# Second block's gates computed with the weights stationary, its attention and retention outputs transposed by background steps

## The chip, the cores and the metric

The kernel runs on one core of one Trainium2 chip. The metric is the device time of one execution in microseconds (us), the median of three runs. The engines are PE (matmuls), DVE (vector), ACT (scalar), POOL and SP (here mostly the queue that issues the weight DMAs).

## What is computed

The input is one sequence of 256 tokens with 1024 features. Two blocks with two layers each run one after the other, all in float32. The first block (a state space mixer and a dilated attention beside each other, then a feed-forward part) is not touched except for the sums of squares at its very end. A layer of the second block is:

```
h = rms_norm_2(x, norm_g[i])
proj = h @ w_in[i]
rq, rk, rv, rz, mq, mk, mv, mz = jnp.split(proj, cuts, axis=-1)     # 512 columns each
r_out = retention(rotary(rq), rotary(rk), rv, ret_norm_g[i])
r_out = jax.nn.silu(rz) * r_out
m_out = moba(rms_norm(mq), rms_norm(mk), mv, rel_bias)
m_out = jax.nn.silu(mz) * m_out
x = x + jnp.concatenate([r_out, m_out], axis=-1) @ w_out[i]
gate = jax.nn.sigmoid(rms_norm_2(x) @ w_ple_gate[i])
x = x + gate * rms_norm_2(p[i] @ w_ple[i], ple_norm_g[i])
```

The gates are the two factors `silu(rz)` and `silu(mz)`, 256 tokens by 512 features each.

## The kernel before

**Products in three parts.** Every large product is split for accuracy: each operand is a rounded high part and a low remainder, and three matmuls (high by high, high by low, low by high) are added in PSUM. The weights come from memory in 488 units of 128 x 1024 values, two units per DMA. ACT makes the high part `wh` of a unit (L154), DVE the low part `wl` (L157; POOL some of them in the first block). Three pairs of `wh` and `wl` exist, and a unit is split two units ahead of its use, so unit n+3 has to wait until PE is done with unit n.

**Two forms of a product.** `slab` (kind "B", L396 to L398 by way of `mmB_unit`) holds 128 tokens of the activations stationary and streams 512 columns of weights: 12 matmuls of 512 columns for a unit; the result has the tokens on the partitions. `pairA` (kind "A", L449 to L451) holds 128 x 128 weights stationary and streams 256 tokens: 24 matmuls of 256 columns for a unit; the result has the features on the partitions. `outT` (L433 to L435) is of the second kind as well, for the output products; its units go through the k blocks in the order (4, 6, 0, 2) for `w_out_2`, so that the first two units read features 512 to 1023 (attention), and the next two features 0 to 511 (retention).

**Order of the work.** The program's text gives an order, in which background steps (generators in `self.bg`) are advanced by one step after each unit (`tick`), and `drain` runs them to the end. A scheduler then orders each engine's instructions by its own estimate of times; on the chip each engine runs its list strictly in that order. PSUM has three banks for products (`mm`), three for small products (`ch`) and two for transposes (`tr`).

**Second half of a layer of the second block.** After the projections for queries, keys and values, `moba` (attention) and `retention` run as background steps and leave their results `ym` and `yr` with tokens on the partitions. The slab of section 7 gives the attention's gate `zm`, that of section 3 the retention's gate `zr`: for each half of the tokens ACT takes the tanh (L889), DVE makes the gate of it (L890). `gated` multiplies `ym` or `yr` by its gate on DVE (L996), transposes the product on PE, four 128 x 128 transposes (L385) for each half of the tokens, and splits it out of PSUM on ACT (L378) and DVE (L389) into the tiles `A` (attention) and `O` (retention), which `w_out_2` reads. For the attention this runs in the background of section 3's slab. For the retention everything is issued after the drain, straight ahead of `w_out_2`.

**Retention.** Two pairs of heads; for a pair: scores (L966, L967) into `ch` banks, decay on DVE (L969), three products a head (L976 to L978), statistics on DVE (L981, L982), a power on POOL (L371), normalising on DVE (L987) and the gain on POOL (L990).

**Norm at the end of the first block.** `Norm.part` adds squares of the features; the norm between the blocks has `first` set and keeps two such sums (n = 0 and n = 1). The last additions (f = 6) are on DVE (L206, L208). `factor` adds over the partitions on PE (L232), `broadcast` spreads the factor by PE (L223), and DVE applies it (L262).

Of the kernel before, what the change touches and what calls it, by code (L numbers as in the profile page):

```python
# [10 lines left out]
F32 = mybir.dt.float32  # L11
F32R = mybir.dt.float32r
BF16 = mybir.dt.bfloat16
AF = mybir.ActivationFunctionType
ALU = mybir.AluOpType
# [3 lines left out]
P = 128  # L19
S = 256  # L20
D = 1024
# [19 lines left out]
QK_BUFS = 4  # L41
# [15 lines left out]
def plan():  # L57

    u = []

    def slab(name, layer, k, c0, kind="B"):
        for r in range(k // 256):
            u.append((kind, name, layer, 256 * r, c0))

    def col(name, layer, c0, k=1024):
        for r in range(0, k, 1024):
            u.append(("A", name, layer, r, c0))  # L70

    def out(name, l):
        for i in range(len(blocks(name)) // 8):
            u.append(("K", name, l, i, 0))

    for l in range(DEPTH):
        out("w_ple_2", l)
    for l in range(DEPTH):
        for half in range(2):
            slab("w_in", l, D, C_V + 512 * half)  # L80
        for half in range(2):
            for c in (C_K, C_Q, C_Q + 1024, C_Q + 2048):
                for f in range(4):
                    col("w_in", l, c + 512 * half + 128 * f)
        for f in range(8):
            col("w_in", l, C_B + 128 * f)
        for g in range(4):
            for f in range(4):
                col("w_in", l, C_XS + 512 * g + 128 * f)
            for f in range(4):  # L90
                col("w_in", l, C_Z + 512 * g + 128 * f)
            for f in range(4 * (g % 2), 4 * (g % 2) + 4):
                if g < 2:
                    col("w_in", l, C_GA + 128 * f)
                else:
                    col("w_attn_branch", l, 128 * f)
        for f in range(8):
            col("w_in", l, C_GS + 128 * f)
        for f in range(8):
            col("w_ssd_branch", l, 128 * f, 2048)  # L100
        out("w_out", l)
        for p in range(2):
            slab("w_gate_up", l, D, 256 * p, "C")
        for p in range(2, NPAIR):
            for j in (0, 128):
                col("w_gate_up", l, 256 * p + j)
            for j in (0, 128):
                col("w_gate_up", l, FFN + 256 * p + j)
        out("w_down", l)
    for l in range(DEPTH):  # L110
        for s in (6, 4, 5):
            slab("w_in_2", l, D, 512 * s)
        for f in range(8):
            col("w_in_2", l, 128 * f)
        for s in (2, 7, 3):
            slab("w_in_2", l, D, 512 * s)
        out("w_out_2", l)
        out("w_ple_gate_2", l)
    return u


class Weights:
# [40 lines left out]
    def next(self, kind, name, layer, r, c0):  # L163
        assert self.plan[self.at] == (kind, name, layer, r, c0), (self.plan[self.at], (kind, name, layer, r, c0))
        self.split_to(self.at + LEAD)
        h, lo = self.hl.pop(self.at)
        self.at += 1
        w = 128 if kind in "AK" else 512
        return h.rearrange("p (k c) -> p k c", c=w), lo.rearrange("p (k c) -> p k c", c=w)


class Norm:
# [13 lines left out]
    def get(self, k):  # L186
        return self.uh[k // 4], self.ul[k // 4], k % 4
# [4 lines left out]
    def part(self, f, n=2):  # L192

        nc = self.net.nc
        h = self.h[:, f:f + 2, :]
        uh, ul = self.uh[f // 4][:, f % 4:f % 4 + 2, :], self.ul[f // 4][:, f % 4:f % 4 + 2, :]
        for n, (acc, new) in enumerate(self.sq):
            q = new if f else acc
            if n == 0:
                nc.scalar.activation(q, h, AF.Square)  # L200
            else:
                for i in range(2):
                    nc.scalar.activation(q[:, i, :], h[:, i, :], AF.Square,
                                         scale=self.first[0][:, f + i:f + i + 1])
            if f:
                (nc.vector if f == 6 else nc.gpsimd).tensor_tensor(acc, acc, new, ALU.add)  # L206
            if f == 6:
                nc.vector.tensor_tensor(acc[:, 0, :], acc[:, 0, :], acc[:, 1, :], ALU.add)  # L208
        if self.gain is None:
            self.net.split(uh, ul, h)  # L210
            return
        for i in range(2):
            g = self.gain[:, f + i:f + i + 1]
            nc.scalar.activation(uh[:, i, :], h[:, i, :], AF.Identity, scale=g)
            nc.vector.scalar_tensor_tensor(ul[:, i, :], h[:, i, :], g, uh[:, i, :].bitcast(F32), ALU.mult,
                                           ALU.subtract)
# [66 lines left out]
class Net:  # L283
# [117 lines left out]
    def slab(self, name, layer, c0, kk, get, kind="B"):  # L401

        n = kk // 256
        ps = [self.mm.tile([P, 512], F32, tag="mm", name="mm") for _ in range(2)]
        for j in range(n):
            hw, lw = self.w.next(kind, name, layer, 256 * j, c0)
            xh, xl, k0 = get(2 * j)
            for t in range(2):
                self.mmB_unit(ps[t], t, hw, lw, xh, xl, k0, j == 0, j == n - 1)
            self.tick()  # L410
        yield from enumerate(ps)
# [578 lines left out]
            nc.gpsimd.tensor_tensor(y[:, :, cs], y[:, :, cs], gain[:, None, cs].to_broadcast([P, 2, 256]), ALU.mult)  # L990
            yield

    def gated(self, y, z, yh, yl):

        for t in range(2):
            self.nc.vector.tensor_tensor(y[:, t, :], y[:, t, :], z[:, t, :], ALU.mult)  # L996
        yield
        for t in range(2):
            ps = self.transpose4([y[:, t, 128 * i:128 * i + 128] for i in range(4)])
            ts = slice(128 * t, 128 * t + 128)  # L1000
            self.split(yh[:, :, ts], yl[:, :, ts], ps.rearrange("p (i t) -> p i t", i=4))

    def ple(self, l):

# [43 lines left out]
    def block2(self, l, x, n1):  # L1048
        nc, a, sp = self.nc, self.a, self.sp
# [6 lines left out]
        def tile(tag, shape, bufs=1):  # L1056
            return sp.tile([P, *shape], F32, tag=tag, name="b2", bufs=bufs)

        qn, qm, qr = [n1.steps()], [], []
# [8 lines left out]
        getu = n1.getv  # L1068
        mk = tile("B1", [4, S])
        self.proj2(l, 5, getu, "k", mk, qm, hg[:, 1, :])  # L1070
        ym, yr = tile("xs", [2, 512], 2), tile("xs", [2, 512], 2)
# [6 lines left out]
        self.proj2(l, 2, getu, "v", rv)  # L1078
        qr.append(self.retention(rq, rk, rv, rg, yr))
        ys = [self.pair([P, 4, S], "O0", "O1"), self.pair([P, 4, S], "A0", "A1")]  # L1080
        zm = tile("A2", [2, 512])
        self.proj2(l, 7, getu, "z", zm)
        qm.append(self.gated(ym, zm, *ys[1]))
        zr = tile("A4", [2, 512])
        self.proj2(l, 3, getu, "z", zr)
        self.drain(qm, qr)
        qr.append(self.gated(yr, zr, *ys[0]))
        next(qr[0])
        e = [sp.tile([P, 4, S], F32, tag=f"B{t}", name="e") for t in range(2)]
        for t in range(2):  # L1090
            nc.sync.dma_start(e[t], self.es[l][:, 4 * t:4 * t + 4, :])
# [151 lines left out]
```

## Time and profile before

| what | value |
|---|---|
| median of 3 runs | 1578.91 us (1575.67 to 1579.48) |
| the profiled execution's own time | 1579.01 us |
| its span, first to last instruction | 1577.2 us |
| mean granted TensorE clock | 0.993 of full speed |
| PE busy | 1540.3 us, 98% of the span |
| DVE busy | 1160.2 us, 74% |
| ACT busy | 822.9 us, 52% |
| POOL busy | 463.6 us, 29% |

Times in the rows are counted from the span's start. The second block runs from about 1253 us to the end; its two layers take some 165 us each. A matmul's row has its start and its modelled length; matmuls overlap, so the pace of PE is read from the distance of two starts. What stands in square brackets at a row's end is the time that the engine was idle before it, and the instruction that ended the wait.

### The profile page before, as it was taken

The numbers are of one execution on the slowest core, as the hardware profiler recorded it, in microseconds if no ns is written. First come the engines' busy times: TensorE is split into PE (matmuls) and PEld (weight loads), VectorE is DVE, ScalarE is ACT, GpSimd is POOL, SyncE is SP. The second block draws the span as 40 slices with busy tenths as digits, with TensorE's granted clock in tenths as the row PEclk, the third lists the DMA queues.
The fourth block names the chain that finished last, engine by engine and source line by source line (L and its number), as shares of the span: only waits on it lengthen the run. The fifth ranks groups of instructions, "written<-read, shape, count | busy, mean of one in ns | idle before, by whom it ended". The sixth has DMA issues, their size and how long they took to land.

```text
span 1577.2 us, 28986 instructions
## 1 busy us (share of the span) xinstructions
PE 1540.3 (98%) x11912; PEld 1467.8 (93%) x11912; DVE 1160.2 (74%) x1760; ACT 822.9 (52%) x1268; POOL 463.6 (29%) x283
## 2 busy tenths in 40 slices
PE   8999999999999999999999999999999999999998
PEld 7999999889989999899998999998999979898988
DVE  7988998775676655668997886677565677788776
ACT  6545577454455444544466764455444554365433
POOL 4666266543000000075436565010000111111110
PEclk9999999999999999999999999999999999999999
DMA  8644444445545555654444455565555545355542
GB/s 306 230 171 153 170 161 167 150 151 206 187 161 187 187 188 187 214 188 161 147 161 148 173 192 194 189 208 197 187 188 186 173 156 183 136 186 175 180 139 96
DMA packets 42660, 280.65 MB, mean 178 GB/s; under 512 B 4864, under 2 KB 7040, under 8 KB 10016
## 3 DMA queue, kind: packets, MB, share of 16 engines
q1 hardware_dynamic: 40592, 267.20, 49.0%
q0 software_dynamic: 1936, 11.60, 1.9%
q8 instruction: 93, 1.52, 0.4%
q14 instruction: 39, 0.32, 0.1%
HBM read 274.53 MB, written 4.26 MB: 177 GB/s over the span
## 4 chain that ended last, share of the span: by engine, by line
PE 85%; DVE 9%; ACT 2%; issue 2%; POOL 1%; DMA 0%; DVEq 0%; SPq 0%; POOLq 0%; ACTq 0%
PE mm L449 17%; PE mm L451 16%; PE mm L450 16%; PE mm L434 6%; PE mm L435 6%; PE mm L433 6%; PE mm L397 4%; PE mm L396 4%; PE mm L398 4%; DVE wl L157 3%; PE ch L662 2%; PE tr L385 1%; ACT wh L154 1%; DVE acc L612 1%; DVE E L525 1%
## 5 line engine op out<-in xcount | busy, mean ns | idle before, releaser
L154 ACT CAST wh<-raw 128x1024 fp32r<-128x1024 f32 x488 | 511.0, 1049 | 587.2 <-PE mm L450 365.1
L157 DVE TENSOR_TENSOR wl<-raw,wh 128x1024 fp32r<-128x1024 f32 x456 | 603.8, 1327 | 273.4 <-ACT wh L154 270.6
L451 PE MATMUL mm<-uh,wl 128*128 128x256 f32 x2112 | 591.7, 280 | 3.8 <-DVE wl L157 3.7
L449 PE MATMUL mm<-uh,wh 128*128 128x256 f32 x2112 | 595.1, 282 | 0.0
L450 PE MATMUL mm<-ul,wh 128*128 128x256 f32 x2112 | 589.5, 279 | 0.0
L449 PEld LDWEIGHTS mm<-uh,wh 128*128 128x128 f32 x2112 | 398.8, 189 | 5.1 <-issue 3.8
L451 PEld LDWEIGHTS mm<-uh,wl 128*128 128x128 f32 x2112 | 397.5, 188 | 5.2 <-DVE wl L157 4.6
L450 PEld LDWEIGHTS mm<-ul,wh 128*128 128x128 f32 x2112 | 398.6, 189 | 0.4 <-issue 0.2
L206 POOL TENSOR_TENSOR nsq<-nsq 128x512 f32<-128x512 f32 x18 | 28.2, 1570 | 474.7 <-ACT nsq L200 407.7
L157 POOL TENSOR_TENSOR wl<-raw,wh 128x1024 fp32r<-128x1024 f32 x32 | 79.1, 2471 | 67.6 <-ACT wh L154 62.5
L433 PE MATMUL mm<-A,wh 128*128 128x256 f32 x288 | 81.5, 285 | 1.4 <-ACT wh L154 1.4
L435 PE MATMUL mm<-A,wl 128*128 128x256 f32 x288 | 81.3, 285 | 0.1
L397 PE MATMUL mm<-wl,nu 128*128 128x512 f32 x192 | 76.5, 400 | 2.7 <-DVE wl L157 2.6
L652 POOL TENSOR_TENSOR M<-M,cb 128x768 f32<-128x768 f32 x32 | 70.0, 2204 | 25.7 <-ACT M L651 17.7
L398 PE MATMUL mm<-wh,nu 128*128 128x512 f32 x192 | 75.3, 395 | 0.0
L396 PE MATMUL mm<-wh,nu 128*128 128x512 f32 x192 | 72.1, 398 | 3.0 <-DVE tg L825 2.2
L470 POOL TENSOR_TENSOR qT<-qT,rp 64x512 f32<-64x512 f32 x32 | 63.1, 1971 | 28.3 <-DVE rp L467 28.2
L612 DVE SCALAR_TENSOR_TENSOR acc<-mm,feat,acc 128x255 f32<-128x255 f32 (+1 forms) x144 | 67.2, 475 | 4.3 <-ACT acc L610 2.9
L469 POOL TENSOR_TENSOR qT<-qT,rot 64x512 f32<-64x512 f32 x32 | 57.2, 1786 | 43.4 <-ACT qT L465 43.4
L434 PE MATMUL mm<-A,wh 128*128 128x256 f32 x224 | 63.6, 285 | 0.0
L433 PEld LDWEIGHTS mm<-A,wh 128*128 128x128 f32 x288 | 55.1, 191 | 1.9 <-ACT wh L154 1.7
L435 PEld LDWEIGHTS mm<-A,wl 128*128 128x128 f32 x288 | 54.6, 191 | 0.6 <-DVE wl L157 0.6
(307 smaller groups left out, 3100.6 us busy)
## 6 DMA issues: line engine op xcount, KB each, us to landing
raw<-in_w_dram SPq DMA_DIRECT2D x243, 1024.0 KB, 4.8
abc<-scr POOLq DMA_DIRECT2D x8, 1024.0 KB, 5.4
es<-e POOLq DMA_DIRECT2D x4, 512.0 KB, 4.2
e<-es SPq DMA_DIRECT2D x4, 512.0 KB, 4.2
raw<-in_w_dram SPq DMA_DIRECT2D x2, 512.0 KB, 4.4
h<-in_xT_dram SPq DMA_DIRECT2D x2, 512.0 KB, 8.9
h<-in_xT_dram SPq DMA_DIRECT2D x1, 1024.0 KB, 4.8
hs<-h POOLq DMA_DIRECT2D x1, 1024.0 KB, 5.9
```

The costliest lines, as they stand in the source:

```text
L154: self.nc.scalar.copy(h, raw)
L157: eng.tensor_tensor(lo, raw, h.bitcast(F32), ALU.subtract)
L396: nc.tensor.matmul(ps, xh[:, k0 + k, ts], hw[:, k, :], start=start and k == 0, stop=False)
L397: nc.tensor.matmul(ps, xh[:, k0 + k, ts], lw[:, k, :], start=False, stop=False)
L398: nc.tensor.matmul(ps, xl[:, k0 + k, ts], hw[:, k, :], start=False, stop=stop and k == 1)
L433: nc.tensor.matmul(ps, hw[:, n % 8, :], xh[:, kx, :], start=opens, stop=False)
L434: nc.tensor.matmul(ps, hw[:, n % 8, :], xl[:, kx, :], start=False, stop=False)
L435: nc.tensor.matmul(ps, lw[:, n % 8, :], xh[:, kx, :], start=False, stop=left[f] == 0)
L449: nc.tensor.matmul(ps, hw[:, k, :], xh[:, kx, :], start=j == 0 and k == 0, stop=False)
L450: nc.tensor.matmul(ps, hw[:, k, :], xl[:, kx, :], start=False, stop=False)
L451: nc.tensor.matmul(ps, lw[:, k, :], xh[:, kx, :], start=False, stop=j == n - 1 and k == 7)
L612: nc.vector.scalar_tensor_tensor(acc[:, j, k:S], ps[:, j, 0:S - k], w[:, 3 - k:4 - k], acc[:, j, k:S], ALU.mult, ALU.add)
```

## The change

The gates are no longer made by `slab` but by `pairA`, two feature blocks at a time, so that they come out with the features on the partitions. `turned` is a new background step list: it transposes the ungated `ym` or `yr` (one half of the tokens a step) and copies it out of PSUM on ACT into `yT`. `gated` now appends `turned` to the queue, runs the two pairs of the gate's product, takes the tanh and makes the gate, drains the queue, multiplies the gate by `yT` and splits the result. It is called once for the attention (section 7) and once for the retention (section 3). The plan of the weights follows: sections 7 and 3 are laid out as columns instead of slabs, with the same number of units in the same place. Beside that, the last additions of the second sum of squares (n = 1) in the norm between the blocks move from DVE to POOL.

```diff
-        for s in (2, 7, 3):
-            slab("w_in_2", l, D, 512 * s)
+        slab("w_in_2", l, D, 1024)
+        for s in (7, 3):
+            for f in range(4):
+                col("w_in_2", l, 512 * s + 128 * f)
...
-                (nc.vector if f == 6 else nc.gpsimd).tensor_tensor(acc, acc, new, ALU.add)
+                (nc.vector if f == 6 and n == 0 else nc.gpsimd).tensor_tensor(acc, acc, new, ALU.add)
             if f == 6:
-                nc.vector.tensor_tensor(acc[:, 0, :], acc[:, 0, :], acc[:, 1, :], ALU.add)
+                (nc.gpsimd if n else nc.vector).tensor_tensor(acc[:, 0, :], acc[:, 0, :], acc[:, 1, :], ALU.add)
...
-    def gated(self, y, z, yh, yl):
-
-        for t in range(2):
-            self.nc.vector.tensor_tensor(y[:, t, :], y[:, t, :], z[:, t, :], ALU.mult)
-        yield
+    def turned(self, y, yT):
+
         for t in range(2):
             ps = self.transpose4([y[:, t, 128 * i:128 * i + 128] for i in range(4)])
-            ts = slice(128 * t, 128 * t + 128)
-            self.split(yh[:, :, ts], yl[:, :, ts], ps.rearrange("p (i t) -> p i t", i=4))
+            self.nc.scalar.copy(yT[:, :, 128 * t:128 * t + 128], ps.rearrange("p (i t) -> p i t", i=4))
+            yield
+
+    def gated(self, l, s, get, y, q, yT, yh, yl):
+
+        nc = self.nc
+        zs = []
+        q.append(self.turned(y, yT))
+        for f in (0, 2):
+            ps = self.pairA("w_in_2", l, 512 * s + 128 * f, D, get)
+            z = self.sp.tile([P, 2, S], F32, tag="qk", name="z", bufs=QK_BUFS)
+            nc.scalar.activation(z, ps, AF.Tanh, scale=0.5)
+            nc.vector.scalar_tensor_tensor(z, z, 1.0, ps, ALU.add, ALU.mult)
+            zs.append((f, z))
+        self.drain(q)
+        for f, z in zs:
+            nc.vector.tensor_tensor(z, z, yT[:, f:f + 2, :], ALU.mult)
+            self.split(yh[:, f:f + 2, :], yl[:, f:f + 2, :], z)
...
-        zm = tile("A2", [2, 512])
-        self.proj2(l, 7, getu, "z", zm)
-        qm.append(self.gated(ym, zm, *ys[1]))
-        zr = tile("A4", [2, 512])
-        self.proj2(l, 3, getu, "z", zr)
-        self.drain(qm, qr)
-        qr.append(self.gated(yr, zr, *ys[0]))
-        next(qr[0])
+        self.gated(l, 7, getu, ym, qm, tile("A2", [4, S]), *ys[1])
+        self.gated(l, 3, getu, yr, qr, tile("A4", [4, S]), *ys[0])
```

What the scheduler makes of it on PE, first layer, where the retention's output `yr` (tile b_14420) is transposed (c_80 holds the identity matrix). Before, it stands between the last matmul on `A` and the first on `O`:

```order
L433 MATMUL mm<-A_14858,wh 128x256
L434 MATMUL mm<-A_14859,wh 128x256
L435 MATMUL mm<-A_14858,wl 128x256
L385 MATMUL tr<-c_80,b_14420 128x128 x8
L433 MATMUL mm<-O_14856,wh 128x256 x4
L434 MATMUL mm<-O_14857,wh 128x256
```

After, the last four of the eight transposes stand eight matmuls ahead of the end of the gate's product (the other four in two pairs further ahead; two lines were added above, so L385 is now L387, and L449 to L451 are L451 to L453):

```order
L451 MATMUL mm<-uh,wh 128x256
L387 MATMUL tr<-c_80,b_14420 128x128 x4
L452 MATMUL mm<-ul,wh 128x256
L453 MATMUL mm<-uh,wl 128x256
...
L435 MATMUL mm<-A_14858,wh 128x256
L436 MATMUL mm<-A_14859,wh 128x256
```

Between the two places stand the last pair of the gate's matmuls and all that reads `A`; nothing but matmuls is left between `A` and `O`.

On ACT, same place. `wh` is the high part of a unit, L889 and L1010 the gate's tanh, L378 and L380 the high part of `O`. Before:

```order
L889 ACTIVATE b_15015<-mm 128x512 x2
L154 CAST wh<-raw 128x1024 x3
L378 CAST O_14856<-tr 128x4x128 x2
L154 CAST wh<-raw 128x1024 x2
L200 ACTIVATE nsq<-h_11769 128x512
```

After:

```order
L1010 ACTIVATE z<-mm 128x512
L156 CAST wh<-raw 128x1024
L999 COPY b_15083<-tr 128x4x128 x2
L156 CAST wh<-raw 128x1024
L1010 ACTIVATE z<-mm 128x512
L380 CAST O_14856<-z 128x512 x2
L156 CAST wh<-raw 128x1024 x4
```

The copies of the transposed `yr` (b_15083) now stand ahead of the split of the third unit of `w_out_2` and of the second pair's tanh, and the high part of `O` is taken from the gated tile `z`.

On DVE, same place. `wl` is the low part of a unit, L890 and L1011 make the gate, L996 and L1015 multiply, L389 and L391 make the low part of `O`. Before:

```order
L987 TENSOR_SCALAR b_14420<-ch,mv,rr 128x128 x4
L890 SCALAR_TENSOR_TENSOR b_15015<-b_15015,mm 128x512 x2
L157 TENSOR_TENSOR wl<-raw,wh 128x1024
L996 TENSOR_TENSOR b_14420<-b_14420,b_15015 128x512 x2
L157 TENSOR_TENSOR wl<-raw,wh 128x1024 x2
L389 TENSOR_TENSOR O_14857<-tr,O_14856 128x4x128 x2
```

After:

```order
L1011 SCALAR_TENSOR_TENSOR z<-z,mm 128x512
L159 TENSOR_TENSOR wl<-raw,wh 128x1024
L1015 TENSOR_TENSOR z<-z,b_15083 128x512
L159 TENSOR_TENSOR wl<-raw,wh 128x1024
L1011 SCALAR_TENSOR_TENSOR z<-z,mm 128x512
L391 TENSOR_TENSOR O_14857<-z,O_14856 128x512
L1015 TENSOR_TENSOR z<-z,b_15083 128x512
L391 TENSOR_TENSOR O_14857<-z,O_14856 128x512
L159 TENSOR_TENSOR wl<-raw,wh 128x1024 x3
```

The two halves of the gate are now the two pairs of feature blocks: the first is multiplied while the second is still to come, and the splits of the units stand between them.

## Rows read from the trace of the kernel before

**Rows 1.** The page's first part: busy us (share of the span) x instructions.

```profile
PE 1540.3 (98%) x11912; PEld 1467.8 (93%) x11912; DVE 1160.2 (74%) x1760; ACT 822.9 (52%) x1268; POOL 463.6 (29%) x283
```

**Rows 2.** Stretches: length, busy us per engine, granted clock, DMA share, GB/s.

```profile
1372.00:1376.00 4.00, 4.00 (x23) 4.00 (x23) 0.00 (x0) 0.44 (x1) 0.00 (x0) 0.58 0.30 127
1376.00:1384.00 8.00, 8.00 (x69) 8.00 (x69) 6.82 (x9) 4.69 (x7) 1.36 (x1) 1.00 0.40 131
```

**Rows 3.** PE around the start of `w_out_2`: start, us, engine, line, operation [idle before].

```profile
1367.30 0.29 PE L435 MATMUL mm<-A,wl 128*128 128x256 f32 x1
1367.43 1.04 PE L385 MATMUL tr<-c,b 128*128 128x128 f32 x8
1369.80 0.74 PE L433 MATMUL mm<-O,wh 128*128 128x256 f32 x4 [1.33 <-ACT O L378]
1371.48 0.39 PE L434 MATMUL mm<-O,wh 128*128 128x256 f32 x1 [0.94 <-DVE O L389]
...
1372.12 0.41 PE L435 MATMUL mm<-O,wl 128*128 128x256 f32 x1
...
1375.48 0.28 PE L433 MATMUL mm<-O,wh 128*128 128x256 f32 x1
...
1378.35 0.28 PE L433 MATMUL mm<-A,wh 128*128 128x256 f32 x1
...
1524.48 0.29 PE L435 MATMUL mm<-A,wl 128*128 128x256 f32 x1
...
1535.53 0.29 PE L433 MATMUL mm<-A,wh 128*128 128x256 f32 x1
```

**Rows 4.** ACT and DVE in the same place, first layer.

```profile
1361.87 0.60 ACT L889 ACTIVATE b<-mm 128x512 f32<-128x512 f32 x1 [0.78 <-PE mm L398]
...
1366.78 1.99 ACT L154 CAST wh<-raw 128x1024 fp32r<-128x1024 f32 x2 [3.38 <-PE mm L434]
1368.68 1.06 ACT L378 CAST O<-tr 128x512 fp32r<-128x512 f32 x2
...
1367.86 2.36 DVE L157 TENSOR_TENSOR wl<-raw,wh 128x1024 fp32r<-128x1024 f32 x2 [1.50 <-ACT wh L154]
1370.14 1.28 DVE L389 TENSOR_TENSOR O<-tr,O 128x512 fp32r<-128x512 f32 x2
```

**Rows 5.** PE's pace: ten steps of 256 columns, twelve of 512 columns.

```profile
1317.86 0.28 PE L450 MATMUL mm<-ul,wh 128*128 128x256 f32 x1
...
1319.01 0.28 PE L451 MATMUL mm<-uh,wl 128*128 128x256 f32 x1
...
1323.21 0.39 PE L396 MATMUL mm<-wh,uh 128*128 128x512 f32 x1
...
1325.96 0.62 PE L396 MATMUL mm<-wh,uh 128*128 128x512 f32 x2
```

**Rows 6.** Retention's last pair of heads, and the gain on POOL (min/median/max ns).

```profile
1356.18 0.39 PE L978 MATMUL ch<-b,sT 128*128 128x128 f32 x2
...
1362.78 1.30 POOL L990 TENSOR_TENSOR b<-b,rg 128x512 f32<-128x512 f32 x1 [2.91 <-DVE b L987]
...
L990 POOL TENSOR_TENSOR b<-b,rg x4: 1299/2013/2723, 1351.1 to 1520.0; 128x512 f32<-128x512 f32 x4
```

**Rows 7.** The norm between the blocks: POOL, PE and DVE.

```profile
1240.48 3.23 POOL L206 TENSOR_TENSOR nsq<-nsq 128x512 f32<-128x512 f32 x2 [13.85 <-ACT nsq L200]
...
1255.27 1.29 DVE L206 TENSOR_TENSOR nsq<-nsq 128x512 f32<-128x512 f32 x2
...
1261.81 0.95 PE L232 MATMUL ch<-ones,nsq 128*128 128x1 f32 x8
...
1269.84 3.22 DVE L262 SCALAR_TENSOR_TENSOR nv<-h,g,ch 128x256 f32<-128x256 f32 x8 [2.24 <-PE ch L223]
...
1277.21 0.50 PE L397 MATMUL mm<-wl,nu 128*128 128x512 f32 x1 [1.87 <-DVE wl L157]
...
1280.33 0.50 PE L397 MATMUL mm<-wl,uh 128*128 128x512 f32 x1 [0.53 <-DVE wl L157]
```

## The prediction, made before the changed kernel ran

> **What bounds the kernel now.** I read the busy times first, then the stretches with PE's idle time and clock, then PE, ACT and DVE side by side where PE stands. PE is busy for 1540.3 of 1577.2 us [rows 1]: the time changes only where PE waits, runs at half clock or gets other work. One such place is in the path of the change: the start of `w_out_2`, once in each layer. The reader is to see there [rows 3]: the last matmul on the attention's half starts at 1367.30, then come the eight transposes of the retention's output (1.04 us), 1.33 us idle until ACT has the high part of `O`, four matmuls, 0.94 us idle until DVE has the low part. Right behind that the matmuls, busy without a gap, lie 0.21 us apart: the 16 steps from 1372.12 to 1375.48 take 3.36 us. The granted clock there is 0.58 on the mean of 4 us, so mostly the lower of the two levels (1.2 GHz), against 1.00 right after [rows 2]. What PE did before it fell was to wait twice within 4 us.
>
> **What the change takes away.** From the last matmul on `A` (1367.30) to the first on `A` in the third quarter (1378.35) are 11.05 us, with 48 matmuls on `O`. At full pace (24 steps from 1375.48 to 1378.35 in 2.87 us, 0.1196 each) 49 steps take 5.86 us, so 5.19 us are extra; 1.04 of it are the transposes, which remain on PE (in groups of 2, 2 and 4 among the gate's matmuls, at about the same 0.13 us each). That leaves **4.15 us a layer**: 2.27 of idle time, 16 x (0.210 - 0.1196) = 1.45 of slow clock, the rest the refilling of PE. The second layer shows the same 11.05 us (1524.48 to 1535.53). Two layers: **-8.3 us**, if no other wait takes the place.
>
> **Does one take it?** Let T be the start of `w_out_2` on PE. Its first half on `A` is 48 matmuls as before, and the order runs 36 of them, then 3 on `O`, then the 12 whose bank the second gate pair held, then the other 45 on `O`. Prices [rows 4]: tanh 0.60, `wh` 1.0, a copy or split out of PSUM on ACT 0.53, `wl` 1.2, low part on DVE 0.64; for a gate or product on DVE, of the same size, I take 0.64 as well.
> - PE: last four transposes end 8 matmuls ahead, at T - 0.9.
> - ACT in its order: two copies of `yr` until T + 0.25, `wh` of the third unit until 1.3, tanh of the second pair until 1.9, high part of the first half of `O` until 2.4.
> - DVE: product of the first half at 0.9, `wl` of the third unit until 2.5, second gate until 3.15, low part of the first half 3.8, second product 4.4; ACT then makes its high part (5.0), DVE its low part (5.7).
> - PE wants the first high part of `O` at 36 x 0.12 = 4.3 (there at 2.4), the bank of the second pair at 4.7 (free at 3.15), the low part at 6.1 (there at 3.8). The third unit's successor needs the first unit's buffer, which PE gives back at about 5.4; ACT and DVE take 1.0 + 1.2 us and are done at 7.8; PE wants it at 8.6, and the second half of `O` as well (5.7).
>
> The smallest slack is 0.8 us, so I count no new wait. What now hides the tail of the gate is the attention's half of `w_out_2`, 5.7 us of PE; without it those 5.7 us a layer would stand open. Further ahead, the transposes want the retention's gain. Before, its last products start at 1356.18 and POOL is done with the gain at 1364.08, 7.9 us later [rows 6]. After, 66 matmuls and four transposes lie between the products and the last transposes, 66 x 0.117 + 0.5 = 8.2 us. That is the thinnest place: 0.3 us, on the pace of before. It may be better, because one low part of `A` instead of two then stands in between on DVE, or worse, because POOL's gain takes from 1.30 to 2.72 us [rows 6].
>
> The Trainium skill (SBUF — State Buffer, section SBUF: two separate sides) says that DVE with two inputs from SBUF and POOL exclude each other on one pair of ports for a whole instruction. The spread of the gain would fit that, though these rows don't show who held whom. By the rule the gain would wait for the `wl` that DVE starts at the same time, which makes the first rival likelier and leaves the sum as it is.
>
> **Gates feature by feature.** Eight units a layer change their form. With 512 columns twelve steps take 2.75 us (1323.21 to 1325.96), which is a unit [rows 5]. With 256 columns ten steps on the same `uh` and `ul` take 1.15 us, 24 of them 2.76; at the pace of `w_out_2` they take 2.87 [rows 3]. I take 0.117, nearer to the rows with the same operands: 2.81, so 0.06 x 16 units = **+0.9 us** (+0.2 to +1.9). The weight loads double in number; they run beside the matmuls, though without room to spare (8.00 busy of 8.00 us) [rows 2].
>
> The Trainium skill (TensorE: Matmul & The Clock Gate, section Back-to-back issue gap) speaks against this step: matmul and weight load together set the pace, 81 ns at 128 columns and 131 ns at 512, so halving the columns does not halve the time. An estimate between its two figures, 98 ns at 256, gives 24 x 98 - 12 x 131 = 0.78 us a unit, 12.5 us in all, and 1582.6 us for the kernel. The trace differs: 229 ns at 512 and 115 at 256.
>
> **Other edits.** Four copies a layer are new on ACT, 2.1 us, beside ACT's waits for PE (3.38 us before one `wh` alone) [rows 4]; nothing on the path, by the chain above. The attention's transposes move forward by a few us of PE and stay hidden. DVE's work for the gates stays at four gates, four products and four low parts. The weights' DMAs keep number, size and order.
>
> **The norm between the blocks.** Two additions go from DVE to POOL: 1.6 us (3.23 for two), and an estimated 0.8 for the half-sized one [rows 7]. DVE ran its additions from 1255.27 to 1256.56, so the input is there by 1256 and POOL ends at about 1258.4, some 3 us before PE reads the sum (1261.81, and 0.5 us earlier in the new order): hidden. The order then puts the broadcast six matmuls of 512 columns earlier, 1.4 us, and DVE's long run (from 1269.84) with it; but two more updates of `h` (0.40 each, as L262 of the same size) and one low part (0.64) now stand ahead of the first `wl`, 1.4 us. So the wait of 1.87 us stays and that of 0.53 us goes [rows 7]: **-0.6 us** (-1.2 to +1.2).
>
> **Sum**: -8.3 + 0.9 - 0.6 = -8.0 against this execution's 1579.0 us (span 1577.2 and 1.8 around it), 0.1 above the median: **1571 us**.
>
> **Rivals.**
> 1. *One wait a layer comes back, the clock holds.* The last transposes wait for POOL's gain, or `O`'s unit for ACT: 1.5 us and 0.3 of refilling. For: a slack of 0.3 us and POOL's spread. Against: DVE reaches the normalising sooner. 2 x 1.8 less gain: 1574.6 us (1573 to 1577).
> 2. *The wait comes back with the slow clock.* 2 us idle, 0.3 refilling, 1.45 of half clock, 3.75 a layer: 1578.5 us. For: the same 2.3 us of idle time brought the clock down before. Against: the idle time would have to be as long again.
> 3. *Slower: the score banks.* Retention's fourth score product takes the `ch` bank of the first head's output, free when DVE has normalised it (L987), which stands behind statistics, POOL's power and the `wl` of a gate unit. In the order PE comes to it fifty matmuls, 5.9 us, after that head's products. If DVE is late by more, PE stands there, in the middle of the gate, and the tail slides too. With 3 us idle, 0.3 and 1.45 a layer: 2 x 4.75 - 8.0 = +1.5, 1580.5 us. It decides for slower from 2.3 us idle a layer; with 5 us idle it is 1584.
> 4. *Slower: the loads set the pace.* With loads at 100% [rows 2], 256 columns might go at 0.150 us instead of 0.117: 16 x 24 x 0.033 = +12.7, 1583.7 us; slower from 0.138. Against: both rows with 256 columns [rows 3, 5]. By the skill's figures above, the same sign.
>
> **How the numbers follow.** Forecast 0.62 (1568.5 to 1573.5), rival 1 0.19, rival 2 0.10, rival 3 0.06, rival 4 0.03. The range goes from 1568 to 1578: it leaves out the slower rivals, half of rival 2 and the forecast's low end. A measurement of this kernel can tell about 0.3%, 4.7 us: faster means below 1574.2. That is the forecast and a quarter of rival 1, 0.67; same is the rest of rival 1, most of rival 2 and a little of rival 3, 0.25; slower 0.08.
>
> **What would show it.** Right: no idle row between `A` and `O` at the start of `w_out_2` in either layer and a clock of 1.00 there; 0.115 to 0.120 us a step in the gate's matmuls; the first transposes of `yr` among them. Wrong: a matmul on `O` waiting for ACT, transposes waiting for POOL's gain, score products waiting for DVE inside section 3's gate, or steps above 0.125 us. If PE has no wait there and the time is still above 1577, the loss is elsewhere, first in the norm between the blocks.

## The result and the profile after

The changed kernel took 1569.7 us (median of 14 runs, 1566.4 to 1576.6) against 1579.0 for the kernel before (14 runs, 1575.7 to 1591.5): ratio 0.9941, 95% interval 0.9925 to 0.9957, so 9.3 us less (6.8 to 11.8). The forecast was 1571 us, with a range from 1568 to 1578. A second measurement beside other kernels gave 1570.5 us, ratio 0.9946 (0.9928 to 0.9964).

The profiled execution was the slowest of the 14 (1576.6 us). Its second block began at 1258.02 us, 5.05 later than in the profile before (1252.97), behind code that is the same. So PE's total says nothing here, and everything below is compared by stages inside the second block. The page's first part, as [rows 1]:

```profile
PE 1541.3 (98%) x12104; PEld 1478.2 (94%) x12104; DVE 1163.3 (74%) x1758; ACT 826.6 (52%) x1276; POOL 462.5 (29%) x285
```

192 more matmuls on PE: 16 units with 24 steps instead of 12. PE around the start of `w_out_2`, to be laid beside [rows 3] (start, us, line, operation, count; lines after the change are two higher; idle time would stand in brackets):

```profile
1361.64 0.28 PE L453 MATMUL mm<-uh,wl 128*128 128x256 f32 x1
...
1362.12 0.38 PE L387 MATMUL tr<-c,b 128*128 128x128 f32 x2
...
1365.64 0.28 PE L453 MATMUL mm<-uh,wl 128*128 128x256 f32 x1
...
1366.77 0.28 PE L451 MATMUL mm<-uh,wh 128*128 128x256 f32 x1
1366.89 0.60 PE L387 MATMUL tr<-c,b 128*128 128x128 f32 x4
...
1368.27 0.28 PE L435 MATMUL mm<-A,wh 128*128 128x256 f32 x1
...
1372.58 0.52 PE L435 MATMUL mm<-O,wh 128*128 128x256 f32 x3
1372.94 0.28 PE L435 MATMUL mm<-A,wh 128*128 128x256 f32 x1
...
1374.37 0.28 PE L435 MATMUL mm<-O,wh 128*128 128x256 f32 x1
...
1379.79 0.36 PE L435 MATMUL mm<-A,wh 128*128 128x256 f32 x1
```

From the first matmul of `w_out_2` to the first on `A` in the third quarter are 11.52 us (1368.27 to 1379.79); before they were 16.68 (1361.67 to 1378.35, the first from this row of before, the second in [rows 3]):

```profile
1361.67 0.40 PE L433 MATMUL mm<-A,wh 128*128 128x256 f32 x2
```

No row has a bracket, the list of PE's waits from 1330 to 1380 us is empty, and so is that from 1485 to 1540 us for the second layer. The stretch (length, busy us and count of PE, PEld, DVE, ACT, POOL, granted clock, DMA share, GB/s), as [rows 2]: where 0.58 stood, 1.00 stands.

```profile
1372.00:1376.00 4.00, 4.00 (x36) 4.00 (x35) 2.28 (x3) 2.62 (x3) 0.00 (x0) 1.00 0.01 4
```

The chain that these matmuls hide, ACT, DVE and POOL in the same place (it answers to [rows 4, 6]):

```profile
1364.38 2.20 POOL L992 TENSOR_TENSOR b<-b,rg 128x512 f32<-128x512 f32 x1 [1.48 <-DVE b L989]
...
1367.31 1.07 ACT L999 COPY b<-tr 128x512 f32<-128x512 f32 x2 [1.04 <-PE tr L387]
...
1369.30 0.59 ACT L1010 ACTIVATE z<-mm 128x512 f32<-128x512 f32 x1
1369.79 0.61 ACT L380 CAST O<-z 128x512 fp32r<-128x512 f32 x1
...
1371.17 0.69 DVE L391 TENSOR_TENSOR O<-z,O 128x512 fp32r<-128x512 f32 x1
1371.77 0.69 DVE L1015 TENSOR_TENSOR z<-z,b 128x512 f32<-128x512 f32 x1
1373.15 0.69 DVE L391 TENSOR_TENSOR O<-z,O 128x512 fp32r<-128x512 f32 x1 [0.69 <-ACT O L380]
```

With T = 1368.27, the first high part of `O` is there at T + 2.1 and the first matmul on it at T + 4.3; the first low part at T + 3.6. POOL is done with the gain at 1366.58, and the last four transposes start at 1366.89: 0.31 us of room.

The norm between the blocks, against [rows 7]: one wait, 2.08 us, where 1.87 and 0.53 stood, and behind it the clock at 0.70, mostly the lower level; at the same place before there was no fall. Below stand the wait, the stretch behind it in the changed kernel, and the stretch at that place in the kernel before:

```profile
1282.26 0.50 PE L399 MATMUL mm<-wl,nu 128*128 128x512 f32 x1 [2.08 <-DVE wl L159]
```

```profile
1283.00:1288.00 5.00, 5.00 (x17) 3.98 (x16) 2.87 (x5) 3.07 (x17) 1.00 (x1) 0.70 0.86 264
...
1278.00:1283.00 5.00, 4.39 (x18) 2.98 (x17) 4.62 (x8) 3.84 (x17) 0.83 (x1) 1.00 0.61 210
```

**The stages of all kernels.** Each number is a difference of two starts of rows on PE: "norm" from the block's first matmul on `nu` to the attention's first score product, "gate" from there to the start of `w_out_2`, "w_out" from there to its end (the first matmul of the next projection on `nu`). The block is the time from the first of these to the end of the last matmul of the program.

| kernel | norm | gate, layer 1, 2 | w_out, layer 1, 2 | block |
|---|---|---|---|---|
| before | 52.75 | 55.95, 55.94 | 28.10, 28.13 | 318.66 |
| before_again | 53.92 | 55.95, 55.94 | 28.07, 28.09 | 319.87 |
| after | 53.29 | 56.96, 56.96 | 23.01, 23.02 | 311.18 |
| after_again | 53.20 | 56.97, 56.96 | 23.01, 23.02 | 311.12 |
| gates_only | 54.07 | 56.96, 56.96 | 23.02, 23.02 | 311.64 |
| norm_only | 53.15 | 55.95, 55.94 | 26.60, 27.84 | 317.33 |
| att_only | 52.80 | 55.99, 55.99 | 25.96, 25.96 | 314.54 |
| ret_only | 54.09 | 56.83, 56.82 | 25.66, 25.65 | 316.86 |
| late_turn | 52.78 | 56.73, 56.72 | 23.06, 23.06 | 310.19 |
| clock_fill | 52.79 | 55.95, 55.94 | 26.59, 26.60 | 315.55 |
| gain_twice | 54.11 | 56.49, 56.48 | 23.59, 23.58 | 312.08 |
| best_late | 50.51 | 57.29, 56.72 | 23.06, 23.07 | 308.44 |
| best_new | 49.09 | 57.28, 56.72 | 23.08, 23.07 | 307.07 |

### The profile page after: what moved, and what is told of

Its sections match the earlier page's. It is cut to its first block, busy times and chain, and to the rows that moved or that the text cites. A ratio compares the mean times of both kernels' runs of the same rounds, so it can differ in the third digit from the quotient of the medians.

```text
span 1574.8 us, 29400 instructions
## 1 busy us (share of the span) xinstructions
PE 1541.3 (98%) x12104; PEld 1478.2 (94%) x12104; DVE 1163.3 (74%) x1758; ACT 826.6 (52%) x1276; POOL 462.5 (29%) x285
## 4 chain that ended last, share of the span: by engine, by line
PE 85%; DVE 8%; ACT 2%; issue 2%; POOL 2%; DMA 1%; DVEq 0%; SPq 0%; POOLq 0%; ACTq 0%
PE mm L451 17%; PE mm L453 17%; PE mm L452 17%; PE mm L435 6%; PE mm L436 6%; PE mm L437 6%; PE mm L399 3%; PE mm L398 3%; PE mm L400 3%; DVE wl L159 2%; PE ch L664 1%; PE tr L387 1%; ACT wh L156 1%; DVE acc L614 1%; DVE E L527 1%
## 5 line engine op out<-in xcount | busy, mean ns | idle before, releaser
L453 PE MATMUL mm<-uh,wl 128*128 128x256 f32 x2240 | 629.3, 281 | 5.8 <-DVE wl L159 3.7
L451 PE MATMUL mm<-uh,wh 128*128 128x256 f32 x2240 | 633.2, 283 | 0.1
L452 PE MATMUL mm<-ul,wh 128*128 128x256 f32 x2240 | 627.5, 280 | 0.0
L453 PEld LDWEIGHTS mm<-uh,wl 128*128 128x128 f32 x2240 | 422.9, 189 | 7.3 <-DVE wl L159 4.6
L451 PEld LDWEIGHTS mm<-uh,wh 128*128 128x128 f32 x2240 | 422.6, 189 | 5.1 <-issue 3.5
L452 PEld LDWEIGHTS mm<-ul,wh 128*128 128x128 f32 x2240 | 425.0, 190 | 0.7 <-issue 0.3
L472 POOL TENSOR_TENSOR qT<-qT,rp 64x512 f32<-64x512 f32 x32 | 60.1, 1877 | 28.3 <-DVE rp L469 28.1
```

What stands on the lines that cost most here:

```text
L451: nc.tensor.matmul(ps, hw[:, k, :], xh[:, kx, :], start=j == 0 and k == 0, stop=False)
L452: nc.tensor.matmul(ps, hw[:, k, :], xl[:, kx, :], start=False, stop=False)
L453: nc.tensor.matmul(ps, lw[:, k, :], xh[:, kx, :], start=False, stop=j == n - 1 and k == 7)
```

## The experiments

**gates_only: the change without the norm edit.**

```diff
-                (nc.vector if f == 6 and n == 0 else nc.gpsimd).tensor_tensor(acc, acc, new, ALU.add)
+                (nc.vector if f == 6 else nc.gpsimd).tensor_tensor(acc, acc, new, ALU.add)
...
-                (nc.gpsimd if n else nc.vector).tensor_tensor(acc[:, 0, :], acc[:, 0, :], acc[:, 1, :], ALU.add)
+                nc.vector.tensor_tensor(acc[:, 0, :], acc[:, 0, :], acc[:, 1, :], ALU.add)
```

> The change without its edit to the norm between the blocks (both additions back on DVE). Theory: the whole gain sits at the start of w_out_2. In the profile of after the stretch from the start of w_out_2 to the third quarter's A is 11.53 us a layer instead of 16.68, and the gate stage ahead of it is 1.02 us longer, so -4.14 a layer; the norm edit cost 0.5 us there (PE waits 2.08 us for DVE's wl and the clock falls to 0.66 on the mean of 5 us). Expected: 1579.0 - 8.3 = 1570.7 by the sum of stages, within 0.6 us of after on either side, and on PE the two waits of 1.87 and 0.53 us as before. Rival: the norm edit gives 0.6 us as predicted, then this kernel is 0.6 us slower than after.

1570.0 us, ratio 0.9946 (0.9927 to 0.9965): the whole gain without the edit. Gate and w_out stand in the table as in after. What was not expected: the norm stage, the code of before again, took 54.07 us instead of 52.75. The stretches show why; first gates_only, then late_turn (below), whose code is the same there:

```profile
1277.00:1282.00 5.00, 3.13 (x12) 2.10 (x11) 5.00 (x11) 3.18 (x5) 0.00 (x0) 0.97 0.01 2
1282.00:1287.00 5.00, 5.00 (x17) 3.92 (x17) 4.17 (x7) 3.20 (x17) 0.90 (x1) 0.69 0.68 221
```

```profile
1273.00:1278.00 5.00, 3.14 (x14) 2.04 (x13) 5.00 (x12) 3.69 (x6) 0.00 (x0) 1.00 0.00 2
1278.00:1283.00 5.00, 4.37 (x18) 2.99 (x17) 4.61 (x9) 3.84 (x17) 0.39 (x1) 1.00 0.59 210
```

PE is idle for as long in both (3.13 and 3.14 busy of 5 us, a wait of 1.87 us), and the clock behind it fell in the one and held in the other. That is 1.3 us which the instructions don't settle.

**norm_only: the kernel before with the norm edit alone** (the diff above, the other way).

> The kernel before with the norm edit alone (both additions of the scaled squares on POOL). Prediction: -0.6 us. What the four runs so far show: the norm stage without the edit lasts 52.75 us in two of them and 54.1 in two others, with the same wait of 1.87 us, the difference being the granted clock behind the wait (1.00 or 0.69 over 5 us); with the edit it took 53.29, with one wait of 2.08 us and the clock down. Theory: the edit takes one of two waits (0.53 us) and lengthens the other by 0.2, so -0.3 us at the same clock and up to +1.4 when the clock falls; a total between -0.6 and +1 us, no difference that can be measured. Rival: the edit makes the fall of the clock regular, then +0.5 to +1.4 us.

1579.6 us, ratio 0.9988 (0.9972 to 1.0003): nothing that can be measured. Three profiles have the edit and the old updates of `h` (after, after_again, norm_only): one wait of 2.1 us and a lowered clock each time, 53.15 to 53.29 us. Eight have neither edit nor best_late's (the two of before, gates_only, att_only, ret_only, late_turn, clock_fill, gain_twice): four with the clock up, 52.75 to 52.80, four with it down, 53.92 to 54.11; 53.4 on the mean. So the edit gave 0.2 us on the mean. Where the clock fell on both sides it gave 0.8 (53.2 against 54.05 on the means). In the three profiles with it the clock fell each time; with odds of four in eight that happens once in eight by chance, so it isn't shown that the edit makes the fall regular.

norm_only showed something else. Its `w_out_2` is that of before, with the same two waits in both layers, 1.33 and 0.94 us. The stretches behind them, first layer, then second:

```profile
1370.00:1374.00 4.00, 3.36 (x28) 3.36 (x29) 0.59 (x1) 0.78 (x1) 0.00 (x0) 1.00 0.54 225
...
1526.00:1530.00 4.00, 3.65 (x20) 3.65 (x21) 0.29 (x1) 0.00 (x0) 0.00 (x0) 0.60 0.51 211
```

28 matmuls at the upper level, 20 at mostly the lower one. The stage took 26.60 us where the clock held and 27.84 where it fell.

**before_again: does the clock fall there every time?** The kernel is before, unchanged.

> The kernel before once more, to see whether the slow clock behind the two waits of 1.33 and 0.94 us at the start of w_out_2 comes every time. Theory (from norm_only, where the same two waits brought the clock down in the second layer and not in the first): the waits are the same to 0.05 us in both layers, and the stretch from the start of w_out_2 to its end takes 28.1 us where the clock fell and 26.6 where it did not; the norm stage 52.8 or 54.1 us by the same chance. Rival: the fall belongs to the instructions and their waits, then 28.1 in both layers as in the first profile.

It fell in both layers, 28.07 and 28.09 us, as the rival had it; but norm_only's first layer stands, so that five of the six passages with these two waits ended in the lower clock. In the norm stage this execution had a fall (53.92 us; 0.66 over 1278 to 1283 us) where the first profile of before had none, with the same wait of 1.87 us.

**clock_fill: PE is given work in the place of the idle time.** The 18 transposes repeat a part of `y`, and nobody reads them.

```diff
+        if fill:
+            ps = self.ch.tile([P, 512], F32, tag="ch", name="ch")
+            for i in range(FILL):
+                self.nc.tensor.transpose(ps[:, 0:128], y[:, 1, 0:128], self.ident)
```

> The kernel before, with 18 transposes of 128 columns more on PE behind the eight of the retention's output (their result is not read): about 2.3 us of work in the place of the 2.27 us of idle time, once a layer. The chain over ACT and DVE stays. Theory (1.45 us a layer of the 4.15 are the lower clock that follows the idle time): from the start of w_out_2 to its end 28.1 - 1.45 = 26.6 us a layer, clock 1.00 there, -2.9 us against before in all; if the filling is longer than the chain by 0.3 us, -2.3. Rival (the slow matmuls have another cause than the idle time ahead of them): 28.1 us a layer as before or longer, 0 to +1 us.

```profile
1367.27 1.03 PE L386 MATMUL tr<-c,b 128*128 128x128 f32 x8
1368.14 2.13 PE L1006 MATMUL ch<-c,b 128*128 128x128 f32 x18
1370.02 0.71 PE L434 MATMUL mm<-O,wh 128*128 128x256 f32 x4
1371.32 0.38 PE L435 MATMUL mm<-O,wh 128*128 128x256 f32 x1 [0.58 <-DVE O L390]
```

```profile
1370.00:1374.00 4.00, 3.42 (x29) 3.22 (x28) 1.26 (x3) 0.11 (x1) 0.00 (x0) 1.00 0.70 252
```

26.59 and 26.60 us, 1.5 less a layer, though PE has 1.9 us more to do (1368.14 to 1370.02): the work stands where PE was idle, and the clock holds. Timed, 1577.3 us, ratio 0.9984 (0.9969 to 0.9999). With one passage of before in six holding its clock unaided, two of two here are strong support, not proof.

**att_only and ret_only: one section each the new way.** The other section keeps its slab, its projection and the old `gated`, with the plan of the weights to match.

```diff
-        self.gated(l, 3, getu, yr, qr, tile("A4", [4, S]), *ys[0])
+        zr = tile("A4", [2, 512])
+        self.proj2(l, 3, getu, "z", zr)
+        self.drain(qm, qr)
+        qr.append(self.gated_old(yr, zr, *ys[0]))
+        next(qr[0])
```

```diff
-        self.gated(l, 7, getu, ym, qm, tile("A2", [4, S]), *ys[1])
+        zm = tile("A2", [2, 512])
+        self.proj2(l, 7, getu, "z", zm)
+        qm.append(self.gated_old(ym, zm, *ys[1]))
```

> Only section 7 (the attention's gate) is made feature by feature; section 3 has the old gate, with products, transposes and splits behind it. Norm as before. In the order the old transposes now stand 21 and 6 matmuls ahead of the first matmul on O instead of directly ahead of it. Theory A (what counts is where PE's queue holds the transposes): the idle time and the slow clock shrink; the first O still waits for ACT's second split, which stands behind two wh, by 0 to 2 us a layer. Against before -3 to -8 us. Theory B (the transposes must leave the chain behind the gate): the stall of 4.15 us stays in both layers, 0 us against before (within 1).

> Only section 3 (the retention's gate) is made the new way; section 7 has the old gate. Norm as before. In the order the last four transposes of the attention's output now stand two matmuls of the gate (0.24 us) ahead of the first matmul on A, and those of the retention's output go behind the third and the 25th matmul on A. Theory (the stall belongs to whichever half of w_out_2 has its transposes right ahead): the stall at O goes, one of 0.5 to 1.4 us a layer appears at the first A, so -8.3 + 1 to 3 = -5.5 us against before, or -3 if the clock falls there too. Rival (only the retention's gate matters): -8.3 us, no wait at A.

1576.5 us, ratio 0.9978 (0.9966 to 0.9989), and 1576.9 us, 0.9977 (0.9968 to 0.9985): 4.4 and 4.0 us less than before beside them, where gates_only had 10.9. PE in att_only, then in ret_only:

```profile
1367.06 0.60 PE L387 MATMUL tr<-c,b 128*128 128x128 f32 x4
...
1369.51 0.60 PE L387 MATMUL tr<-c,b 128*128 128x128 f32 x4
1371.17 0.74 PE L435 MATMUL mm<-O,wh 128*128 128x256 f32 x4 [1.07 <-ACT O L380]
1372.55 0.39 PE L436 MATMUL mm<-O,wh 128*128 128x256 f32 x1 [0.63 <-DVE O L391]
```

```profile
1363.20 0.60 PE L387 MATMUL tr<-c,b 128*128 128x128 f32 x4
...
1364.48 0.62 PE L435 MATMUL mm<-A,wh 128*128 128x256 f32 x3 [0.43 <-ACT A L380]
...
1372.00 0.74 PE L435 MATMUL mm<-O,wh 128*128 128x256 f32 x4 [0.59 <-ACT O L380]
1373.35 0.39 PE L436 MATMUL mm<-O,wh 128*128 128x256 f32 x1 [0.61 <-DVE O L391]
```

In att_only the retention's gate is the old one, and on its side the place of its transposes in PE's queue differs: four stand behind the 31st matmul on `A` and four behind the 48th, where before all eight stood behind the 48th. So the last four are still directly ahead of the first matmul on `O`; the 21 and 6 matmuls of the expectation are not what the trace shows. The waits shrink only from 2.27 to 1.70 us, but the clock held in both layers, and w_out is 2.1 to 2.2 us shorter; some 1.5 of that is the clock, by the 28.1 and 26.6 us above. Theory B is out, since the stall did not stay as it was, though three quarters of its idle time did. Of PE's 1.07 us, the second split of `O` itself takes 0.58 (1370.55 to 1371.13); the 0.44 ahead of it, from the end of the transposes (1370.11), are time in which ACT still had two `wh` to finish (1368.40 to 1370.63). In ret_only the old gate of the attention brings a wait at the first `A`, as expected; that `O` waits as well I had not expected. The last transposes of the retention's output go late there, and on ACT a `wh` (1370.38 to 1371.43) stands between the products' end (1370.91) and the split. The rival's -8.3 us is out. With one section alone moved, 1.6 to 1.7 us a layer stay idle; to lose all of it, both have to move.

att_only also prices the new form of the gate: its gate stage has eight transposes as before and one section with 256 columns instead of 512, and is 0.04 to 0.05 us longer for four units.

**late_turn: the transposes behind the gate's matmuls instead of among them.**

```diff
-        q.append(self.turned(y, yT))
+        if s == 7:
+            q.append(self.turned(y, yT))
...
+        if s == 3:
+            q.append(self.turned(y, yT))
         self.drain(q)
```

> As the change without the norm edit, but the eight transposes of the retention's output stand together behind all matmuls of its gate, directly ahead of w_out_2. Theory (what counts is that no transpose stands between the gate's product and the split, and that the attention's 48 matmuls, 5.7 us, cover copies, second gate, products and splits): chain from the start of w_out_2 is copies until 1.1, products until 2.5, high parts and low parts until about 4.4 us, wanted at 5.7: no wait, -8.3 us as with the transposes ahead. Rival (the transposes have to be ahead of the gate): O waits again, 1 to 2.3 us idle a layer with 1.45 us of slow clock, -1 to -5 us.

1570.7 us, ratio 0.9947 (0.9929 to 0.9965).

```profile
1362.12 1.03 PE L387 MATMUL tr<-c,b 128*128 128x128 f32 x8
1362.91 0.37 PE L435 MATMUL mm<-A,wh 128*128 128x256 f32 x1
...
1368.69 0.64 PE L435 MATMUL mm<-O,wh 128*128 128x256 f32 x4
```

```profile
1365.02 1.29 DVE L1018 TENSOR_TENSOR z<-z,b 128x512 f32<-128x512 f32 x2
1366.39 1.29 DVE L391 TENSOR_TENSOR O<-z,O 128x512 fp32r<-128x512 f32 x2
```

The eight transposes stand directly ahead of `w_out_2`, and still no wait: the last low part is there at 1367.68, and PE comes to `O` at 1368.69. That the retention's transposes run ahead of the gate's matmuls is not what brings the gain; it is that none is left between the gated product and its split, so that PE's 48 matmuls on `A` cover the rest.

**gain_twice: more work in the thinnest link.**

```diff
             nc.gpsimd.tensor_tensor(y[:, :, cs], y[:, :, cs], gain[:, None, cs].to_broadcast([P, 2, 256]), ALU.mult)
+            if h0:
+                nc.gpsimd.tensor_scalar(y[:, :, cs], y[:, :, cs], 1.0, None, op0=ALU.mult)
```

> gates_only with one more pass of POOL over the second half of the retention's output (times 1.0, between gain and transposes), 1.3 to 2.2 us more in the link that had 0.31 us of slack. In the order the last four transposes then stand behind the tenth matmul on A instead of eight matmuls ahead of the first. Theory (the chain behind the gate has room, the first O is wanted 5.7 us behind the start of w_out_2): copies until 2.4, products until 3.7, low parts until 5 us; no wait on PE, as gates_only within 0.6 us. Rival (the thin link decides, rival 1 of the prediction): a wait of 1 to 2 us a layer at the transposes or at O, +2 to +4 us.

```profile
1357.51 2.21 POOL L992 TENSOR_TENSOR b<-b,rg 128x512 f32<-128x512 f32 x1 [1.48 <-DVE b L989]
1359.82 2.35 POOL L994 TENSOR_SCALAR b<-b 128x512 f32<-128x512 f32 x1
```

POOL ends 2.4 us later than with the first pass alone, and the order answers by putting the last four transposes behind the tenth matmul on `A`. PE has no wait at either place in either layer, and gate and w_out together are as long as in gates_only (80.1 us against 80.0). Since the order moved with the longer gain, the run does not show what a late gain would cost in the changed kernel's own order. The median was 1572.8 us (ratio 0.9969, 0.9951 to 0.9986), 2.3 above after_again beside it. The profiled execution was the fastest of the ten (1569.8 us), so its stages do not show where the rest comes from, and that stays open.

**best_late and best_new: the wait in the norm.** The rows of DVE in after name the cause: eight updates of `h` (3.2 us) run ahead of the `wl` that PE waits for until 1282.26, and `h` is next read behind `w_out_2`, at 1379.23.

```profile
1276.64 1.26 DVE L275 SCALAR_TENSOR_TENSOR h<-h,gains,ch 128x256 f32<-128x256 f32 x3
...
1278.42 0.87 DVE L275 SCALAR_TENSOR_TENSOR h<-h,gains,ch 128x256 f32<-128x256 f32 x2
...
1279.81 1.26 DVE L275 SCALAR_TENSOR_TENSOR h<-h,gains,ch 128x256 f32<-128x256 f32 x3
1280.98 1.22 DVE L159 TENSOR_TENSOR wl<-raw,wh 128x1024 fp32r<-128x1024 f32 x1
```

In the two runs here they are held back by an input that comes some 30 us later (0 times a piece of the retention's q).

```diff
-        if self.first:
-            for _ in range(8):
-                yield
-            rb = self.broadcast(self.r1)
...
+    def rest(self, dep):
+        net, nc = self.net, self.net.nc
+        r = net.small(2, "nr1")
+        nc.vector.scalar_tensor_tensor(r, dep, 0.0, self.r1, ALU.mult, ALU.add)
+        rb = self.broadcast(r)
...
         self.proj2_rope(l, 0, getu, rq)
+        if n1.first:
+            qr.append(n1.rest(rq[:, 0, 0:2]))
```

> late_turn with one edit more: the eight updates of h that ended the norm between the blocks on DVE (3.2 us, ahead of the low parts and the first wl) are held back by a true input until the retention's q is there, some 30 us later. Theory: they are what makes PE wait 1.87 us for DVE's wl; without them wl is done 2 us earlier, the wait goes and with it the fall of the clock that follows in some runs: 2 to 3 us less than late_turn, 1570.7 - 2.5 = 1568 us; the updates cost nothing at the new place, where DVE has room. Rival: the wait is ACT's or the weights', then as late_turn.

> best_late with the norm edit as well (both additions on POOL, broadcast five matmuls earlier). Theory: with the updates of h gone the earlier broadcast lets the normalised input come 1.4 us earlier; against best_late 0 to -1 us, and no PE wait in the norm stage. Rival: the edit gives nothing, same as best_late within 0.5 us.

1568.4 us, ratio 0.9918 (0.9900 to 0.9936), and 1566.8 us, 0.9911 (0.9893 to 0.9929). All that PE waits from 1250 to 1310 us, best_late first, then best_new with the stretch of its wait:

```profile
PE mm L401 <- DVE wl L159: 0.8, 1, 0.8
```

```profile
PE mm L400 <- ACT wh L156: 0.2, 1, 0.2
```

```profile
1278.00:1283.00 5.00, 4.76 (x22) 3.55 (x21) 3.57 (x12) 2.57 (x12) 2.01 (x2) 1.00 0.72 244
```

The waits of 1.87 and 0.53 us are gone, but a wait is left in each, where both expectations had none: 0.8 us for DVE's `wl` in best_late, 0.2 for ACT's `wh` in best_new. The norm stage is 50.51 and 49.09 us, and the gate stage of the first layer 0.56 longer than in late_turn, since the broadcast on PE now stands there. With the updates out of the way the norm edit is worth 1.4 us in the profiles; alone it had given nothing that the timing can tell.

The changed kernel and best_new once more, side by side:

> The changed kernel again, beside best_new on the same chip: 1569.7 us as before, 9.3 below the kernel before. Its norm stage ends in one wait of about 2.1 us for DVE's wl, with the clock behind it low or not.

> best_new beside the changed kernel: 2.9 us less by the medians so far (1566.8 against 1569.7). By the stages of the profiles: norm stage 49.1 us against 53.3 (4.2 less), of it 1.4 the clock that does not fall in every run, the start of w_out_2 equal: 2.8 to 4.2 us less. Rival: within 1 us of it.

1570.5 us (1570.1 to 1570.7) and 1567.2 us (1560.8 to 1568.3), ratios to before 0.9946 (0.9928 to 0.9964) and 0.9914 (0.9883 to 0.9946): 3.3 us less by the medians, where the second block is 4.2 shorter (306.88 against 311.12). The four times of best_new here lie below the four of the changed kernel, so it is faster than both kernels of the study.

## Why the prediction was right

- **The stall (-8.3 us).** Right in mechanism and, for the profile it was read from, in size: w_out lost 5.09 and 5.11 us a layer, where the prediction counted 5.19 as extra, and no wait is left there. With the gate stage, which got longer, 4.08 and 4.09 remain a layer, 8.2 in all, against 7.4 by the two terms of the forecast (-8.3 and +0.9). But 1.45 of the 4.15 were the clock, and that fell in five of six passages only. Against the mean of the six, 27.8 us, the gain of both stages is 3.8 a layer, 7.6 in all.
- **No wait takes its place.** The chain came within 0.3 us of the times forecast: first high part T + 2.1 (2.4), first low part 3.6 (3.8), second high part 4.8 (5.0). The thinnest place had 0.31 us (forecast 0.3), but that was luck in part: POOL's gain took 2.20 us instead of the 1.30 it was read from, and started 0.8 us sooner behind the last products (5.8 us, 1358.60 to 1364.38, instead of 6.6). gain_twice shows that even 2.4 us more there need not become a wait, if the last transposes then go behind the start of `w_out_2`. Rivals 1 and 2 did not come, nor rival 3: no score product waited.
- **The gates feature by feature (+0.9 us): mis-sized.** The gate stage grew by 1.01 us a layer, and most of that is the eight transposes that moved there. Together in one group they hold PE for 0.79 us from start to start (late_turn, 1362.12 to 1362.91), and late_turn's stage grew by 0.78; in groups of 2, 2 and 4 the same eight cost more. So two sections of the new form cost nothing there, and the one in att_only cost 0.05. Steps of 256 columns took 0.113 us in one place (ten from 1365.64 to 1366.77) and 0.120 in another (four from 1361.64 to 1362.12), so that 24 of them last about as long as 12 of 0.229. I had taken 0.117 and 2.81 us a unit; the sections show 2.76 or less. Rival 4 is out with it. An estimate between the two figures of the Trainium skill (TensorE: Matmul & The Clock Gate, section Back-to-back issue gap) would have made it 12.5 us dearer; the trace differs, and the trace decides.
- **The norm (-0.6 us): the waits right, the clock missed.** As forecast, the wait of 0.53 us went and the other stayed (2.08 for 1.87). POOL's additions were hidden (done at 1263.05, PE read at 1266.39). The step that failed is that a wait which stays costs what it did: the clock behind it fell, which it had not in the profile before, so this stage came out 0.54 us longer instead of 0.6 shorter. Against the mean of eight profiles it is 0.2 shorter, and 0.8 shorter against the four of them whose clock fell as well.

The sum: -8.0 forecast; in the profiles of the second block 318.66 and 319.87 before, 311.18 and 311.12 after, -8.1 by their means. The medians differ by 9.3 (6.8 to 11.8); the 1.2 us between the two come from outside the second block or from scatter, and I can't say which. That the sum came so near the forecast is in part luck: the gates cost 0.8 us less than forecast, and the norm came out 1.1 worse in the first pair of profiles.

## What to carry to other kernels

When a step that follows PE's last product sits on PE again (a transpose behind a gate), look for a form in which it acts on the other operand, so that only ACT and DVE are left in the tail and the next stage's independent half covers them; where the retention's transposes then stood mattered little here (late_turn, gain_twice). Move all stages that meet there, since one old section left 1.6 to 1.7 us of waits a layer. Before counting on a clock's share of a stall, look at several profiles, and look ahead of a wait on DVE for work that nobody needs yet: putting it off (best_late, 2.3 us of the norm stage) brought more than moving other work around it (the norm edit alone, 0.2 on the mean).

## What was not expected of the hardware

The granted clock behind an idle stretch is not settled by the instructions. The same two waits (1.33 and 0.94 us) ended in the lower level in five of six passages; a wait of 1.87 us in the norm in four of eight, one of 2.08 in three of three, and waits of 1.07 and 0.63 us in none of two. A fall cost 1.1 to 1.5 us.

DVE's short instructions grew beside POOL. While POOL made its two additions (1260.63 to 1263.05 in after), DVE's L217 took 1.52 us and L210 0.96; before, without them, 0.48 and 0.42. The profiles of norm_only, after_again and best_new have 1.52 and 0.96 again.

```profile
1260.63 1.54 POOL L208 TENSOR_TENSOR nsq<-nsq 128x512 f32<-128x512 f32 x1 [11.86 <-ACT nsq L205]
1262.24 0.81 POOL L210 TENSOR_TENSOR nsq<-nsq 128x256 f32<-128x256 f32 x1
...
1260.93 1.52 DVE L217 SCALAR_TENSOR_TENSOR nu<-h,g,nu 128x256 fp32r<-128x256 f32 x1
1262.37 0.96 DVE L210 TENSOR_TENSOR nsq<-nsq 128x256 f32<-128x256 f32 x1
```

That fits what the Trainium skill (SBUF — State Buffer, section SBUF: two separate sides) says, that an instruction of one is held until the other's is done; each of DVE's two ends 0.28 us behind one of POOL's (1262.45 and 1263.33 behind 1262.17 and 1263.05). No run here shows the holding itself.
